# Modulation vectors from unsplit fp32 weights, in four column strips of TensorE

## Chip, cores and metric

One core of a Trainium2 chip runs the whole kernel. The metric is the device time of one execution in microseconds (us). Engines are named as the profile does: PE (TensorE), PEld (its weight loads), DVE (VectorE), ACT (ScalarE), POOL (GpSimd), SP (SyncE, which issues the DMA transfers here).

## What is computed

Two layers over 1024 latent and 256 context tokens of width 1024. Each layer modulates its input by vectors that come from a condition vector `c` (for the latents) and `c_ctx` (for the context), runs attention, a state-space mixer (SSD) and retention side by side, and adds their projection, gated. The part of the reference that matters:

```python
def hybrid_layer(x, ctx, c, c_ctx, w_ada, b_ada, w_in, w_out, ...):
    shift, scale, gate = jnp.split(jax.nn.silu(c) @ w_ada + b_ada, 3, axis=-1)
    ...   # the same for c_ctx; h = rms_norm(x) * (1 + scale) + shift
    ...   # h @ w_in, the mixers, x + gate * (mix @ w_out)
```

`w_ada` is 1024 x 3072 for each of the two layers, in fp32: the product of two vectors (c and c_ctx) with a matrix of 12.6 MB, twice.

## The kernel before

Dense products run with each fp32 operand split into two halves: a rounded one (`hi`, type fp32r, a copy on ACT) and the rest (`lo`, a subtraction on POOL or DVE; `split`, lines 273 to 277). A product then takes three passes, hi x hi, hi x lo and lo x hi (`mm3`, lines 303 and 305).

Weights come in blocks of 256 output columns by 1024 rows (eight contraction tiles of 128). `w_order` writes the order of all blocks by hand, `prefetch` loads the next one, `next_w` hands out the loaded one and asks for the one after it. A block's halves live in tiles `wh` and `wl`, two buffers each. The raw fp32 data come through tiles `raw` (three small buffers), or, for the source marked "gv", through the ring of sixteen large buffers as `wr`; four transfers of 256 KB a block. In the dense stream the splits of a block wait in `pieces` and are let go one at each step of the stream.

The modulation vectors (`ada`, from line 224) are twelve such blocks a layer. The condition is the stationary operand: `sc` holds hi and lo of both vectors as four columns. For each contraction tile `k` and each half `j` of the weights one product of 4 by 256 is accumulated (line 234, sixteen a block); the 4 x 256 result is copied to `adar` on DVE; two small products with `pick` add the four rows in pairs and turn columns into partitions (line 240); one DVE instruction adds the bias (line 243).

In the opening (`run`) the eight blocks of layer 0's shift and scale are made in the order ADA0, and the first chunk of 512 tokens is normalised between them: `norm_h` needs the shift and scale of each feature tile `k` (hu, line 442; ah, line 449; al, line 450, the last also on DVE). Then come the first dense products (`first_dense`), and with them the second chunk of x. The other sixteen blocks (gate of layer 0, all of layer 1) run in the dense stream of layer 0, as LATE says, between weight blocks 10 and 22. The stream is interleaved with the mixers by budgets (SHARE), in which an ada block counts 2.0. Within this order a planner that simulates the engines sets the final order of instructions on each engine, the DMA issues on SP's queue among them.

In the SSD mixer, `pair_stage2` (line 778) multiplies in plain fp32, without a split: two heads alternate, one writing PSUM partitions 0 to 63, the other 64 to 127.

Of the kernel before, what the change touches and what calls it, by code (L numbers as in the profile page):

```python
# [9 lines left out]
F32 = mybir.dt.float32  # L10
# [8 lines left out]
P = 128  # L19
# [21 lines left out]
LAG = 2  # L41
LATE = (1, 0, 1, 3, 2, 2, 2, 2, 1, 1, 1, 1, 3)
PJ = 1
PN = 3
ADA0 = (0, 4, 1, 5, 2, 6, 3, 7)

# [6 lines left out]
class Net:  # L53
# [25 lines left out]

# [1 line left out]
    def nm(self, s):  # L81
# [26 lines left out]

# [1 line left out]
    def copy(self, out, in_, eng=None):  # L110
# [41 lines left out]

# [1 line left out]
    def setup(self):  # L154
# [52 lines left out]

# [1 line left out]
    def silu_c(self):  # L209
        nc = self.nc  # L210
        cc = self.work("cc", (P, KT, 2))
        nc.sync.dma_start(out=cc, in_=self.a["cc"])
        th = self.work("cth", (P, KT, 2))
        nc.scalar.activation(out=th, in_=cc, func=AF.Tanh, scale=0.5)
        nc.vector.scalar_tensor_tensor(out=th, in0=th, scalar=1.0, in1=cc, op0=ALU.add, op1=ALU.mult)
        nc.vector.tensor_scalar(out=th, in0=th, scalar1=0.5, scalar2=None, op0=ALU.mult)
        self.sc = self.const("sc", [P, KT, 4], F32R)
        nc.vector.tensor_copy(out=self.sc[:, :, 0:2], in_=th)
        nc.vector.tensor_tensor(out=self.sc[:, :, 2:4], in0=th, in1=self.sc[:, :, 0:2].bitcast(F32), op=ALU.subtract)
        self.pick = self.const("pick", [4, 2])  # L220
        nc.vector.tensor_tensor(out=self.pick, in0=self.ident[0:4, 0:2], in1=self.ident[0:4, 2:4], op=ALU.add)

    def ada(self, l, ns):
        nc = self.nc
        cols = self.cc_[l][0]
        if l not in self.ada_t:
            self.ada_t[l] = self.c_p.tile([P, 24, 2], F32, tag=f"ada{l}", name=f"ada{l}")
        out = self.ada_t[l]
        for n in ns:
            w = self.next_w()  # L230
            ps = self.pmm()
            for k in range(KT):
                for j in range(2):
                    nc.tensor.matmul(ps[0:4, 0:256], lhsT=self.sc[:, k, :], rhs=w[j][:, k, :],
                                     start=(k == 0 and j == 0), stop=(k == KT - 1 and j == 1))
            row = self.c_p.tile([4, 256], F32, tag="adar", name=self.nm("adar"))
            self.copy(row[0:4, 0:256], ps[0:4, 0:256], "v")
            pt = self.pst()
            for j in range(2):
                nc.tensor.matmul(pt[:, 2 * j:2 * j + 2], lhsT=row[0:4, j * P:(j + 1) * P], rhs=self.pick,  # L240
                                 start=True, stop=True)
            o = out[:, 2 * n:2 * n + 2, :]
            nc.vector.scalar_tensor_tensor(
                out=o, in0=pt[:, 0:4].rearrange("p (j c) -> p j c", c=2), scalar=1.0 if 4 <= n < 8 else 0.0,
                in1=cols[:, COLS["ba"] + 2 * n:COLS["ba"] + 2 * n + 2].unsqueeze(2).to_broadcast([P, 2, 2]),
                op0=ALU.add, op1=ALU.add)
            yield 2.0

# [1 line left out]
    def load_w(self, src, eng="g"):  # L250
        nc = self.nc
        hi = self.w_p.tile([P, KT, 256], F32R, tag="wh", name=self.nm("wh"))
        lo = self.w_p.tile([P, KT, 256], F32R, tag="wl", name=self.nm("wl"))
        self.stage_w(src, hi, lo, 2, eng)
        return hi, lo

    def stage_w(self, src, hi, lo, m, eng="g"):
# [34 lines left out]

# [1 line left out]
    def mm3(self, ps, wh, wl, ah, al, w_first):  # L294
# [63 lines left out]

# [1 line left out]
    def defer(self, n, fn):  # L360
# [37 lines left out]

# [1 line left out]
    def new_act(self, c):  # L400
# [71 lines left out]

# [1 line left out]
    def conv_evac(self, t, idx, cv, edge, c, n, ps):  # L474
# [377 lines left out]

# [1 line left out]
    def rope(self, x):  # L854
# [189 lines left out]

# [1 line left out]
    def ret_mix(self, pr, last):  # L1046
# [83 lines left out]

# [1 line left out]
    def load_mix(self, c, tiles, cols, scaled):  # L1132
# [112 lines left out]

# [1 line left out]
    def w_order(self, l):  # L1247
        wi, wa = self.a["wi"], self.a["wa"]
        q = [(wa[0, i], "gv") for i in ADA0] if l == 0 else []
        late = iter([(wa[0, i],) for i in range(8, 12)] + [(wa[1, i],) for i in range(12)])  # L1250
        for i in range(N_W):
# [7 lines left out]
    def dense_all(self, l, last, cols, cv, xin):  # L1259
# [14 lines left out]
        for j in range(3):  # L1274
            yield from xz(5 + j, 3 + j)
        late = iter([(0, n) for n in range(8, 12)] + [(1, n) for n in range(12)] if l == 0 else [])

# [88 lines left out]
    def run(self):  # L1366
# [7 lines left out]
        for j, n in enumerate(ADA0):  # L1374
# [3 lines left out]
            if j % 2:  # L1378
                next(h0)
                next(h0)  # L1380
            if j == 4:
                self.load_dt(0)
# [27 lines left out]
def _layout(inp):  # L1410
# [6 lines left out]
    o["cc"] = np.stack([g["c"][0].reshape(KT, P).T, g["c_ctx"].reshape(KT, P).T], -1)  # L1417
    o["wa"] = g["w_ada"].reshape(DEPTH, KT, P, 12, 256).transpose(0, 3, 2, 1, 4)

# [71 lines left out]
```

## Time and profile before

| | us |
|---|---|
| median of 3 runs | 2968.34 |
| lowest and highest | 2963.67, 2970.11 |
| span of the profiled execution | 2963.4 |
| PE busy | 2683.0 |
| DVE busy | 1992.9 |
| ACT busy | 1277.0 |
| POOL busy | 1191.2 |

The span goes from the first to the last instruction of one execution; the page gives no other time of that execution. Busy times of engines overlap. Ends of matmuls are modelled, and they are pipelined, so that starts tell more than ends of what a product costs.

### The profile page before, as it was taken

Reading aid. Unit: us, or ns where it says so; the run is one execution under the profiler, and the core shown is the slowest. Engines: PE = TensorE matmul, PEld = TensorE weight load, DVE = VectorE, ACT = ScalarE, POOL = GpSimd, SP = SyncE. Lnnn points to the kernel's source line nnn. Section 1 sums busy time; section 2 is a strip of 40 time slices with the busy share of each in tenths; the row PEclk is TensorE's granted clock in tenths of the full one; section 3 lists DMA queues with packets and bytes.
Section 4 is the critical chain, followed back from the end, with each engine's and each line's share of the span. In section 5 each row is a group of like instructions: output and inputs, shape, how many; then the busy total and the mean of one; then the engine's idle time right before and its main releaser. Section 6 shows DMA issues by size and latency. Waiting matters only on the chain.

```text
span 2963.4 us, 47064 instructions
## 1 busy us (share of the span) xinstructions
PE 2683.0 (91%) x17708; PEld 2352.7 (79%) x17708; DVE 1992.9 (67%) x4409; ACT 1277.0 (43%) x3297; POOL 1191.2 (40%) x910
## 2 busy tenths in 40 slices
PE   6887988779899989998999989997899999999999
PEld 4666777669788879897878777775798888989887
DVE  7668778765767785657445558888658767665651
ACT  5345555443545454523132345545435444452330
POOL 5546656662423231325240336666531211212550
PEclk8988999889999999999999989998999999999999
DMA  6022222221211111204462122222110100001461
GB/s 236 13 69 81 80 76 67 82 67 43 58 44 52 44 53 29 68 27 122 135 216 79 39 73 79 72 78 72 58 43 15 37 15 22 29 24 36 148 211 60
DMA packets 128339, 211.23 MB, mean 71 GB/s; under 512 B 12080, under 2 KB 53232, under 8 KB 128112
## 3 DMA queue, kind: packets, MB, share of 16 engines
q1 hardware_dynamic: 128112, 208.23, 22.5%
q8 instruction: 139, 2.28, 0.3%
q14 instruction: 88, 0.72, 0.1%
HBM read 172.47 MB, written 35.72 MB: 70 GB/s over the span
## 4 chain that ended last, share of the span: by engine, by line
PE 53%; DVE 13%; issue 5%; ACT 3%; DMA 2%; POOL 1%; SPq 0%; DVEq 0%; POOLq 0%; ACTq 0%
PE mm L303 23%; PE mm L305 13%; PE t L149 4%; PE o L975 4%; PE s L924 4%; DVE mx L926 2%; DVE te L747 2%; PE o L778 1%; ACT e L936 1%; DVE e L954 1%; POOL wl L277 1%; DVE mt L744 1%; PE s L710 1%; DMA raw<-in_wi_dram 1%; DVE mt L752 1%
## 5 line engine op out<-in xcount | busy, mean ns | idle before, releaser
L277 POOL TENSOR_TENSOR wl<-raw,wh 128x512 fp32r<-128x512 f32 x288 | 391.5, 1380 | 705.8 <-ACT wh L275 699.0
L303 PE MATMUL mm<-ah,wh 128*128 128x512 f32 (+1 forms) x1680 | 635.3, 378 | 41.2 <-DVE cv L489 7.6
L303 PE MATMUL mm<-al,wh 128*128 128x512 f32 (+1 forms) x1680 | 626.9, 373 | 1.0 <-DVE al L277 1.0
L303 PE MATMUL mm<-ah,wl 128*128 128x512 f32 (+1 forms) x1680 | 626.2, 373 | 0.0
L305 PE MATMUL mm<-wh,ah 128*128 128x256 f32 x1568 | 455.1, 291 | 17.5 <-DVE zu L357 9.9
L305 PE MATMUL mm<-wl,ah 128*128 128x256 f32 x1568 | 451.1, 288 | 0.3 <-POOL wl L277 0.3
L305 PE MATMUL mm<-wh,al 128*128 128x256 f32 x1568 | 450.1, 287 | 0.0
L303 PEld LDWEIGHTS mm<-ah,wh 128*128 128x128 f32 x1680 | 323.9, 193 | 101.9 <-issue 19.4
L303 PEld LDWEIGHTS mm<-ah,wl 128*128 128x128 f32 x1680 | 323.7, 193 | 52.8 <-issue 2.4
L303 PEld LDWEIGHTS mm<-al,wh 128*128 128x128 f32 x1680 | 324.3, 193 | 51.6 <-issue 2.4
L305 PEld LDWEIGHTS mm<-wh,ah 128*128 128x128 f32 x1568 | 302.4, 193 | 24.0 <-DVE zu L357 10.4
L936 ACT ACTIVATE e<-s,nb 128x512 f32<-128x512 f32 (+1 forms) x384 | 231.8, 613 | 198.3 <-DVE nb L931 197.0
L305 PEld LDWEIGHTS mm<-wl,ah 128*128 128x128 f32 x1568 | 302.9, 193 | 4.3 <-issue 1.2
L305 PEld LDWEIGHTS mm<-wh,al 128*128 128x128 f32 x1568 | 302.8, 193 | 3.0 <-issue 0.9
L926 DVE TENSOR_REDUCE mx<-s 128x1 f32<-128x512 f32 (+1 forms) x400 | 223.1, 586 | 64.3 <-PE s L924 63.2
L275 ACT ACTIVATE wh<-raw 128x512 fp32r<-128x512 f32 x288 | 169.1, 625 | 173.1 <-DMA raw<-in_wi_dram 62.0
L924 PE MATMUL s<-kT,qT 128*128 128x512 f32 (+1 forms) x800 | 218.9, 377 | 10.2 <-ACT e L936 8.7
L750 POOL TENSOR_TENSOR mt<-mt,G 128x512 f32<-128x512 f32 x72 | 117.3, 1632 | 177.1 <-DVE mt L744 168.1
L747 DVE SCALAR_TENSOR_TENSOR te<-R,dtpk,te 128x128 f32<-128x128 f32 x288 | 176.0, 656 | 9.5 <-ACT te L739 9.5
L755 POOL TENSOR_TENSOR R<-R,cv 128x1024 f32<-128x1024 f32 x72 | 177.6, 2468 | 2.9 <-ACT R L754 2.9
L975 PE MATMUL o<-v,aT 128*128 128x128 f32 x1312 | 176.4, 277 | 0.7 <-DVE aT L118 0.5
L975 PEld LDWEIGHTS o<-v,aT 128*128 128x128 f32 x1312 | 165.2, 194 | 4.1 <-DVE aT L118 0.9
(265 smaller groups left out, 5182.1 us busy)
## 6 DMA issues: line engine op xcount, KB each, us to landing
raw<-in_wi_dram SPq DMA_DIRECT2D x176, 256.0 KB
R<-cumd SPq DMA_DIRECT2D x72, 512.0 KB
raw<-in_wa_dram SPq DMA_DIRECT2D x64, 256.0 KB
mr<-mix SPq DMA_DIRECT2D x64, 256.0 KB
wr<-in_wa_dram SPq DMA_DIRECT2D x32, 256.0 KB
raw<-in_wo_dram SPq DMA_DIRECT2D x32, 256.0 KB
x<-xr SPq DMA_DIRECT2D x24, 256.0 KB
mix<-cv SPq DMA_DIRECT2D x8, 640.0 KB
```

The costliest lines, as they stand in the source:

```text
L149: self.nc.tensor.transpose(ps[:, j * P:(j + 1) * P], srcs[i + j], self.ident)
L275: nc.scalar.activation(out=hi, in_=x, func=AF.Copy)
L277: e.tensor_tensor(out=lo, in0=x, in1=hi.bitcast(F32), op=ALU.subtract)
L303: nc.tensor.matmul(ps, lhsT=w, rhs=x, start=st, stop=sp)
L305: nc.tensor.matmul(ps, lhsT=x, rhs=w, start=st, stop=sp)
L747: nc.vector.scalar_tensor_tensor(out=te[:, hh, c, :], in0=Rv[:, 1, hh, c, :], scalar=col(self.ncum, c, 1, hh), in1=te[:, hh, c, :], op0=AL ...
L750: nc.gpsimd.tensor_tensor(out=mt, in0=mt, in1=G[:, c0:c0 + 2, :].unsqueeze(1).to_broadcast([P, 2, 2, P]), op=ALU.mult)
L755: nc.gpsimd.tensor_tensor(out=cs, in0=cs, in1=cT[:, tk].unsqueeze(1).to_broadcast([P, 4, 256]), op=ALU.mult)
L924: nc.tensor.matmul(ps[:, 0:n], lhsT=qT[:, 2 * m + s, :], rhs=kT[m][:, t0:t0 + n], start=(s == 0), stop=(s == 1))
L926: nc.vector.tensor_reduce(out=mx[:, ci:ci + 1], in_=ps[:, 0:n], axis=AX.X, op=ALU.max, negate=len(chunks) == 1)
L936: nc.scalar.activation(out=em[:, t0:t0 + n], in_=pss[ci][:, 0:n], func=AF.Exp, bias=nb, accum_out=z[:, 3 * m + ci:3 * m + ci + 1])
L975: nc.tensor.matmul(po[:, 0:P], lhsT=aT[j], rhs=v[:, j, :], start=(j == b0), stop=(j == NT - 1))
```

## The change

The weights of the modulation vectors are no longer split. `load_a` brings a block of 512 columns straight into the buffers of `wh` (contraction tiles 0 to 3) and `wl` (4 to 7), as plain fp32, in four transfers of 512 KB. `sc` holds the two vectors in fp32, padded with zeros to 32 columns. For each half `j` four products go to the four column strips of the array: strip `g` takes contraction tile 4j + g and writes PSUM partitions 32g to 32g + 31. The 128 x 512 result is copied to SBUF, into the ring of work tiles, and four small products with a 128 x 2 `pick` add the strips and turn columns into partitions. There are six blocks a layer in place of twelve; four in the opening, eight in the stream, of which LATE places one at a time. A block counts 2.5 in the budgets. In the opening four feature tiles of h follow each second block.

```diff
-LATE = (1, 0, 1, 3, 2, 2, 2, 2, 1, 1, 1, 1, 3)
+LATE = (1, 0, 1, 1, 1, 1, 1, 1, 1, 0, 0, 0, 0)
-ADA0 = (0, 4, 1, 5, 2, 6, 3, 7)
+ADA0 = (0, 2, 1, 3)
...
-        self.sc = self.const("sc", [P, KT, 4], F32R)
-        nc.vector.tensor_copy(out=self.sc[:, :, 0:2], in_=th)
-        nc.vector.tensor_tensor(out=self.sc[:, :, 2:4], in0=th, in1=self.sc[:, :, 0:2].bitcast(F32), op=ALU.subtract)
-        self.pick = self.const("pick", [4, 2])
+        self.sc = self.const("sc", [P, KT, 32])
+        nc.vector.memset(self.sc, 0.0)
+        nc.vector.tensor_scalar(out=self.sc[:, :, 0:2], in0=th, scalar1=0.5, scalar2=None, op0=ALU.mult)
+        self.pick = self.const("pick", [P, 2])
...
-            for k in range(KT):
-                for j in range(2):
-                    nc.tensor.matmul(ps[0:4, 0:256], lhsT=self.sc[:, k, :], rhs=w[j][:, k, :],
-                                     start=(k == 0 and j == 0), stop=(k == KT - 1 and j == 1))
-            row = self.c_p.tile([4, 256], F32, tag="adar", name=self.nm("adar"))
-            self.copy(row[0:4, 0:256], ps[0:4, 0:256], "v")
+            for j in range(2):
+                for g in range(4):
+                    nc.tensor.matmul(ps[32 * g:32 * g + 32, :], lhsT=self.sc[:, 4 * j + g, :], rhs=w[j][:, g, :],
+                                     start=(j == 0), stop=(j == 1))
+            row = self.work("adar")
+            self.copy(row, ps, "v")
             pt = self.pst()
-            for j in range(2):
-                nc.tensor.matmul(pt[:, 2 * j:2 * j + 2], lhsT=row[0:4, j * P:(j + 1) * P], rhs=self.pick,
+            for j in range(4):
+                nc.tensor.matmul(pt[:, 2 * j:2 * j + 2], lhsT=row[:, j * P:(j + 1) * P], rhs=self.pick,
                                  start=True, stop=True)
...
-            yield 2.0
+            yield 2.5
...
     def load_w(self, src, eng="g"):
+        if eng == "ada":
+            return [self.load_a(src, j) for j in range(2)]
...
+    def load_a(self, src, j):
+        t = self.w_p.tile([P, 4, 512], F32, tag=("wh", "wl")[j], name=self.nm("wa"))
+        for g in range(0, 4, 2):
+            self.nc.sync.dma_start(out=t[:, g:g + 2, :], in_=src[:, 4 * j + g:4 * j + g + 2, :])
+        return t
...
-        q = [(wa[0, i], "gv") for i in ADA0] if l == 0 else []
-        late = iter([(wa[0, i],) for i in range(8, 12)] + [(wa[1, i],) for i in range(12)])
+        q = [(wa[0, i], "ada") for i in ADA0] if l == 0 else []
+        late = iter([(wa[0, i], "ada") for i in (4, 5)] + [(wa[1, i], "ada") for i in range(6)])
...
             if j % 2:
-                next(h0)
-                next(h0)
-            if j == 4:
+                for _ in range(4):
+                    next(h0)
+            if j == 2:
```

## Rows read from the trace of the kernel before

**Rows 1.** The page, part 1: busy us, share of the span, instructions.

```profile
PE 2683.0 (91%) x17708; PEld 2352.7 (79%) x17708; DVE 1992.9 (67%) x4409; ACT 1277.0 (43%) x3297; POOL 1191.2 (40%) x910
```

**Rows 2.** Stretches of the opening: busy per engine, granted clock, DMA share, GB/s.

```profile
12.00:32.00 20.00, 14.77 (x87) 9.09 (x88) 18.52 (x29) 12.37 (x21) 16.00 (x11) 0.91 1.02 356
36.00:40.00 4.00, 2.58 (x22) 1.58 (x20) 4.00 (x8) 3.59 (x7) 1.51 (x2) 1.00 0.68 201
44.00:48.00 4.00, 2.88 (x12) 0.89 (x10) 3.88 (x8) 2.98 (x8) 2.52 (x2) 0.50 0.77 236
48.00:52.00 4.00, 3.13 (x14) 1.82 (x15) 4.00 (x5) 3.68 (x7) 2.84 (x2) 0.50 0.88 254
```

**Rows 3.** Timeline of the opening: start, us, engine, line, operation, out<-in, count.

```profile
29.69 7.69 SPq L263 DMA_DIRECT2D wr<-in_wa_dram  x7
...
57.47 0.28 PE L234 MATMUL mm<-wl,sc 128*4 128x256 f32 x1
...
60.17 1.39 DVE L442 SCALAR_TENSOR_TENSOR hu<-x,ada,s 128x512 f32<-128x512 f32 x2
...
62.09 1.40 DVE L450 SCALAR_TENSOR_TENSOR al<-hu,ada,ah 128x512 fp32r<-128x512 f32 x2
...
66.42 0.62 ACT L410 ACTIVATE acc<-x 128x512 f32<-128x512 f32 x1
```

**Rows 4.** Line 234, 600 to 1260 us: its products; what ended PE's idle time.

```profile
L234 PE MATMUL mm<-wh,sc x128: 276/277/418, 629.3 to 1240.3; 128*4 128x256 f32 x128
...
  DVE zu L357: 11.4, 2
  POOL wl L277: 4.4, 4
...
  ACT wh L275: 2.2, 3
```

**Rows 5.** The stretch of the stream, columns as in group 2.

```profile
700.00:1260.00 560.00, 528.12 (x3796) 480.17 (x3796) 391.45 (x897) 282.99 (x820) 172.69 (x119) 0.97 0.17 50
```

**Rows 6.** Timeline at 18 to 22 us: transposing products, norm sums, one block's products.

```profile
18.67 0.60 PE L240 MATMUL t<-pick,adar 4*128 4x2 f32 x4
...
19.20 1.05 PE L427 MATMUL t<-ones,acc 128*128 128x1 f32 x8
...
20.11 0.28 PE L234 MATMUL mm<-wl,sc 128*4 128x256 f32 x1
...
21.82 0.28 PE L234 MATMUL mm<-wh,sc 128*4 128x256 f32 x1
```

**Rows 7.** Timeline at 310 and 336 us: plain fp32 products in two strips.

```profile
310.16 0.32 PE L778 MATMUL o<-R,st 128*64 128x128 f32 x1
...
310.16 0.32 PE L778 MATMUL o<-mt,xn 128*64 128x128 f32 x1
...
310.32 0.27 PE L778 MATMUL o<-R,st 128*64 128x128 f32 x1
...
336.12 0.39 PE L778 MATMUL o<-mt,xn 128*64 128x128 f32 x4
...
336.34 0.39 PE L778 MATMUL o<-R,sf 128*64 128x128 f32 x4
...
336.88 0.19 PEld L303 LDWEIGHTS mm<-ah,wh 128*128 128x128 f32 x1 [0.17 <-issue]
```

**Rows 8.** 600 to 1260 us: POOL's subtractions by group; ACT's waits before its copies.

```profile
L277 POOL TENSOR_TENSOR wl<-raw,wh 128x512 fp32r<-128x512 f32 x112 | 152.4, 1380 | 319.9 <-ACT wh L275 315.0 <-PE s L924 2.9 <-DMA raw<-in_wa_dram 1.7
...
  DMA raw<-in_wa_dram: 24.4, 22
```

**Rows 9.** DVE copies from PSUM: ns min/median/max of adar; group of aT.

```profile
L118 DVE COPY adar<-mm x16: 402/409/413, 633.3 to 1240.7; 4x256 f32<-4x256 f32 x16
...
L118 DVE COPY aT<-t 128x512 f32<-128x512 f32 x64 | 43.9, 686 | 35.9 <-PE t L149 35.4
```

**Rows 10.** DMA of the first 62 us: packets, bytes, mean rate.

```profile
DMA packets 11236, 17.49 MB, mean 282 GB/s; under 512 B 1760, under 2 KB 3680, under 8 KB 11232
```

More of the change, by code (lines that the diff above doesn't have):

```diff
@@ L215, in silu_c @@
         nc.vector.scalar_tensor_tensor(out=th, in0=th, scalar=1.0, in1=cc, op0=ALU.add, op1=ALU.mult)
-        nc.vector.tensor_scalar(out=th, in0=th, scalar1=0.5, scalar2=None, op0=ALU.mult)
-        self.sc = self.const("sc", [P, KT, 4], F32R)
-        nc.vector.tensor_copy(out=self.sc[:, :, 0:2], in_=th)
-        nc.vector.tensor_tensor(out=self.sc[:, :, 2:4], in0=th, in1=self.sc[:, :, 0:2].bitcast(F32), op=ALU.subtract)
-        self.pick = self.const("pick", [4, 2])
-        nc.vector.tensor_tensor(out=self.pick, in0=self.ident[0:4, 0:2], in1=self.ident[0:4, 2:4], op=ALU.add)
+        self.sc = self.const("sc", [P, KT, 32])
+        nc.vector.memset(self.sc, 0.0)
+        nc.vector.tensor_scalar(out=self.sc[:, :, 0:2], in0=th, scalar1=0.5, scalar2=None, op0=ALU.mult)
+        self.pick = self.const("pick", [P, 2])
+        nc.vector.tensor_reduce(out=self.pick, in_=self.ident.rearrange("p (g c) -> p c g", g=4)[:, 0:2, :],
+                                axis=AX.X, op=ALU.add)
     def ada(self, l, ns):
@@ L231, in ada @@
             ps = self.pmm()
-            for k in range(KT):
-                for j in range(2):
-                    nc.tensor.matmul(ps[0:4, 0:256], lhsT=self.sc[:, k, :], rhs=w[j][:, k, :],
-                                     start=(k == 0 and j == 0), stop=(k == KT - 1 and j == 1))
-            row = self.c_p.tile([4, 256], F32, tag="adar", name=self.nm("adar"))
-            self.copy(row[0:4, 0:256], ps[0:4, 0:256], "v")
+            for j in range(2):
[4 more added lines that the diff above has]
+            self.copy(row, ps, "v")
             pt = self.pst()
-            for j in range(2):
-                nc.tensor.matmul(pt[:, 2 * j:2 * j + 2], lhsT=row[0:4, j * P:(j + 1) * P], rhs=self.pick,
+            for j in range(4):
+                nc.tensor.matmul(pt[:, 2 * j:2 * j + 2], lhsT=row[:, j * P:(j + 1) * P], rhs=self.pick,
                                  start=True, stop=True)
-            o = out[:, 2 * n:2 * n + 2, :]
             nc.vector.scalar_tensor_tensor(
-                out=o, in0=pt[:, 0:4].rearrange("p (j c) -> p j c", c=2), scalar=1.0 if 4 <= n < 8 else 0.0,
-                in1=cols[:, COLS["ba"] + 2 * n:COLS["ba"] + 2 * n + 2].unsqueeze(2).to_broadcast([P, 2, 2]),
+                out=out[:, 4 * n:4 * n + 4, :], in0=pt[:, 0:8].rearrange("p (j c) -> p j c", c=2),
+                scalar=1.0 if 2 <= n < 4 else 0.0,
+                in1=cols[:, COLS["ba"] + 4 * n:COLS["ba"] + 4 * n + 4].unsqueeze(2).to_broadcast([P, 4, 2]),
                 op0=ALU.add, op1=ALU.add)
-            yield 2.0
+            yield 2.5
     def load_w(self, src, eng="g"):
-        nc = self.nc
+        if eng == "ada":
+            return [self.load_a(src, j) for j in range(2)]
         hi = self.w_p.tile([P, KT, 256], F32R, tag="wh", name=self.nm("wh"))
@@ L1275, in dense_all @@
             yield from xz(5 + j, 3 + j)
-        late = iter([(0, n) for n in range(8, 12)] + [(1, n) for n in range(12)] if l == 0 else [])
+        late = iter([(0, n) for n in (4, 5)] + [(1, n) for n in range(6)] if l == 0 else [])
         def more(i):
@@ L1417, in _layout @@
     o["cc"] = np.stack([g["c"][0].reshape(KT, P).T, g["c_ctx"].reshape(KT, P).T], -1)
-    o["wa"] = g["w_ada"].reshape(DEPTH, KT, P, 12, 256).transpose(0, 3, 2, 1, 4)
+    o["wa"] = g["w_ada"].reshape(DEPTH, KT, P, 6, 512).transpose(0, 3, 2, 1, 4)
     def cols(*ranges):
```

## Prediction

> **What bounds the kernel now.** I read the page first: TensorE (PE) is busy 2683 of 2963.4 us, far ahead of VectorE (DVE) with 1993, ScalarE (ACT) with 1277 and GpSimd (POOL) with 1191 [rows 1]. The work that changes stands in two places with different limits, so I read each by itself.
>
> The first is the opening, up to about 63 us, where eight modulation blocks are made, on which the first chunk's dense products wait. The table by stretches shows the loads at 356 GB/s from 12 to 32 us, but at 201 to 254 in the three stretches shown between 36 and 52 us, where DVE is busy nearly all the time and the granted clock falls to 0.5 (the 1.2 GHz level) [rows 2]. The timeline tells why: the last load of modulation weights is issued at 37.4 us, but the last of their products ends at 57.75, and the last of the eight normalised tiles of the first chunk (al, line 450) at 63.5 [rows 3]. So for some 20 us the data are there, and the splits into two halves on ACT, DVE and POOL, the one ring of buffers behind them, and a PE at half clock set the pace. That is no DMA limit.
>
> The second is 629 to 1240 us, where the other sixteen blocks run in the dense stream beside the mixers [rows 4]. From 700 to 1260 us PE is busy 528 of 560 us at a granted clock of 0.97 [rows 5]. There a microsecond of PE work saved is about a microsecond of time, and ACT and POOL work saved is worth only the PE waits that it causes.
>
> **The change, part by part.** The profile's span is 2963.4 us; the runs shown have a median of 2968.3 and a lowest of 2963.7, so some time up to 7 us lies around or beside the profiled execution, and I carry the difference that I work out over to the median.
>
> *Products in the stream, removed.* An old block is 16 products of 256 columns; the sixteen that start from 20.11 to 21.82 stand 1.71 / 15 = 0.114 us apart, so a block is 1.82 us. Two transposing products follow, which the trace shows as four records: 0.53 us from their start to the next instruction's, 18.67 to 19.20 [rows 6]. Sixteen blocks: 16 x 2.35 = 37.6 us of PE.
>
> *Products in the stream, added.* Eight new blocks of eight plain fp32 products, 32 weight columns by 512. No such product is in the trace. The nearest are those of line 778: plain fp32, 64 weight columns by 128, which alternate between the two halves of the array as the new ones alternate between four strips. Each leaves two records, so two passes. The first passes of the two halves both start at 310.16 and the second at 310.32; in steady state a group of four records follows the last after 0.22 us (336.12, 336.34) [rows 7]. So a pass of 128 columns costs 0.109 us, both halves run at once, and a product does not hold up its neighbour's first pass by its own second. Scaled to 512 columns a pass is 0.436 us; a block in four strips is two rounds of two passes, 4 x 0.436 = 1.74 us. Bounds: 0.9 us if the 0.109 is the loading of 64 weight columns and a pass streams at the pace of the old products, 2 x 0.114 for 512 columns [rows 6]; 16 x 0.436 = 7.0 us if the strips do not overlap. I take 1.74, since line 778 is the only plain fp32 work in strips here. To it I add 0.35 us for going into strips and out again (the next full-array product shows 0.17 us of idle weight loading after line 778, at 336.88 [rows 7]; taken twice), and the four transposing products, now over 128 partitions: eight records, which in line 427, also 128 weight columns by a few, take 0.9 us up to the next start, 19.20 to 20.11 [rows 6]. Eight blocks: 8 x (1.74 + 0.35 + 0.90) = 23.9 us. PE saves 13.7 us.
>
> A rule stands against full overlap. The rows of line 778 show two strips in the time of one [rows 7]. The Trainium skill, "TensorE: Matmul & The Clock Gate", Part 3 (packing small matmuls), states 2.38 times for three column strips, and that matmuls start and end strictly in program order. By the first figure four strips would overlap 3.2-fold, an estimate of 2.2 us a block and 2940 us in all; the second, if a product's two passes count as neighbours in the program, is rival B below. On the order, the trace disagrees for two strips: both first passes start together; no run here shows four.
>
> *Splits, removed.* In the stream POOL makes 112 subtractions of 1380 ns, of which 64 belong to these blocks (88 us) and each follows a copy on ACT, which stood 24.4 us waiting for their loads [rows 8]. POOL and ACT are not the bound, so this is worth the PE waits ahead of these products that the splits ended: 4.4 us on POOL and 2.2 on ACT. The 11.4 us put down to DVE zu is a wait for a PSUM bank and remains [rows 4]. Gain 6.6 us, between 0 and, if fewer visits meet fewer waits for the bank, 15.
>
> *Evacuation.* The copy grows from 4 x 256 (0.41 us) to 128 x 512 (0.69 us as in aT) [rows 9]; sixteen become eight, so DVE loses 1 us of work. The products of the mixers cover PE's wait for it, since PE is 94% busy there [rows 5], so I cost it at nothing. Uncovered it is 8 x 0.3 = 2.4 us.
>
> *Loads.* The bytes stay. A block now goes straight into the weight buffers, so its transfers on SP's queue wait until PE has left the block before last, and what is behind them there (the next weights, the mixers' stores) waits too. In the stream a block is asked for one weight block ahead, tens of microseconds, against about 6 us for 2.1 MB at 350 GB/s, so this is hidden. If it were not hidden, it would cost up to 8 x 6 us.
>
> *The opening.* The 32 transfers of wa and 8 of x are 10.5 MB; at 356 GB/s [rows 2] they take 29.5 us, from about 3 us on, so the last block lands at 32.5. Two buffers keep the queue filled: a block lands every 5.9 us and its products, at half clock, take 4 x 0.87 = 3.5. The opening moves 17.49 MB in all [rows 10]; half of the other 7 may be put ahead, which gives 42.5; I take 37. Behind it: half a block of products at half clock 1.7 us, copy 0.7, transposing 1.8, sum 0.2 and hops, together 5; then four tiles of h, now together after the last block, 4 x 1.45 us of DVE as hu and al show [rows 3], with the tail 7. The first chunk is ready at 49 instead of 63.5, between 44.5 and 54.5. What is late next is the second chunk of x: it is read at 66.4 (acc) [rows 3], and all 17.49 MB at 356 GB/s end at 52, against a need 14 us earlier than now, also 52. So I take 12 us, between 4 (these loads or the order of the queue bind) and 18.
>
> Sum: 13.7 + 6.6 + 12 = 32.3 us; 2968.3 - 32.3 = **2936 us**.
>
> **The rivals.** A, the forecast. Its own range: 18 + 13.7 + 15, and the 7 us by which a block's lower bound (0.9) undercuts 1.74 over eight, so 54 us (2914), to 4 + half of 13.7 + 0 (2957).
>
> B, two strips at a time: if the passes go out in program order, a block takes nine slots of 0.436, 3.9 us. Eight blocks with the rest cost 8 x 5.2 = 41.6 us, 4 more than now, which the waits return; in the opening a block at half clock takes 7.9 us, more than the 5.9 of its load, so the opening gains 3. Result 2963, no change. Against it: the two first passes that start together.
>
> C, strips one after another (they share one stream of operands): 8 x (7.0 + 1.25) = 66 us, 28 more than now, less 6.6 of waits; in the opening four blocks of 14 us at half clock end at 70 us instead of 57.75, 12 later. Result 3001, slower. It decides from where the eight products of a block cost over 3.45 us: that is what two old blocks (4.7) less switching and transposing (1.25) leave. Against it: line 778. For it: four strips ask for twice the operands that two did, and no row shows that rate.
>
> D, the gain is made and handed back: the order on every engine is planned anew for the whole program, x comes late in the opening, or the mixers' chains, not PE, set the stream. The opening's 4 and half of 13.7, less some 6 for a worse order: 2963.
>
> **How the numbers follow.** A 0.65, B 0.13, C 0.11, D 0.11. Differences of 0.2% (6 us) are about what a measurement of this kernel can tell from no change. C is slower and D may be by a little: 0.12. Within 0.2%: most of B and D and the slow end of A, 0.15. Faster: 0.73. The range takes A, B and most of D, 2912 to 2966.
>
> **What would show it.** In the profile after: rounds of four records of line 234's successor within some 10 ns, 0.44 us apart at full clock (B: pairs; C: singles); its PE time in the stream about 2 us a block; no wr or raw tile of in_wa, 112 - 64 = 48 POOL subtractions between 600 and 1260 us; the first dense product with the last h tile near 49 us; loads above 300 GB/s up to 40 us. The forecast is wrong if the strips overlap less than twofold, if PE idle rises in the stream by what its work falls, or if the opening still ends after 58 us.

## The result, and the profile after

The changed kernel takes 2937.24 us (median; 2934.35 to 2938.81), against 2969.05 for the kernel before on the same chip: a ratio of 0.990, 95% interval [0.9885, 0.9914]. Predicted were 2936. The profiled execution has a span of 2932.5 us, 30.9 less than before.

In the first part of the page (busy time, share of the span, instructions by engine) every engine has less work than in [rows 1]; GpSimd's falls most, by a tenth:

```profile
PE 2655.7 (91%) x17516; PEld 2323.2 (79%) x17516; DVE 1940.6 (66%) x4368; ACT 1224.5 (42%) x3201; POOL 1074.6 (37%) x830
```

Where the 30.9 us arise can be followed along instructions that both kernels have. The second chunk's first accumulation (acc) starts at 55.4 instead of 66.4 us: 11.0. At the store of the fifth pair of SSD heads 13.3 are gained, 474.9 against 488.2. From there to the end of layer 0, the stage that holds the modulation blocks of the stream, come 17.6 more. Layer 1 adds nothing. The table by stretches shows that stage (length, then busy time and instructions of PE, PEld, DVE, ACT, POOL, then clock, DMA share, GB/s). Before:

```profile
core 0: us, PE busy (x) PEld busy (x) DVE busy (x) ACT busy (x) POOL busy (x), PEclk, DMA share, GB/s
488.18:1544.23 1056.05, 965.02 (x6750) 870.75 (x6750) 702.61 (x1529) 456.73 (x1260) 407.22 (x309) 0.96 0.24 72
```

After:

```profile
474.85:1513.34 1038.49, 944.81 (x6622) 850.33 (x6622) 674.12 (x1510) 419.92 (x1193) 316.41 (x245) 0.95 0.23 73
```

PE's busy time falls by 20.2 us; its idle time, 91.0 and 93.7 us, doesn't fall. DVE loses 28.5 us of busy time with 19 instructions fewer, more than those instructions held: its copies, casts and reductions each take the same time to within 1 us, and the fall lies in TENSOR_TENSOR and SCALAR_TENSOR_TENSOR, which read two tensors (498.5 us before, 469.5 after). It is the first hint of a term that the prediction lacked.

The opening, which answers [rows 2]:

```profile
12.00:32.00 20.00, 16.25 (x78) 6.11 (x80) 8.75 (x28) 2.75 (x5) 0.00 (x0) 0.91 0.99 361
36.00:40.00 4.00, 3.75 (x22) 1.58 (x23) 2.15 (x9) 1.72 (x5) 0.53 (x1) 1.00 1.05 385
40.00:44.00 4.00, 4.00 (x22) 3.15 (x20) 3.96 (x4) 3.22 (x6) 3.88 (x4) 1.00 1.05 387
44.00:48.00 4.00, 0.77 (x3) 0.24 (x2) 3.96 (x8) 2.68 (x5) 1.55 (x1) 1.00 1.06 380
48.00:52.00 4.00, 3.42 (x9) 2.47 (x10) 3.12 (x5) 0.40 (x1) 0.00 (x0) 0.63 0.64 205
```

In these stretches the loads run at 361 to 387 GB/s up to 48 us, where the kernel before fell to 201 to 254. PE has next to nothing to do from 44 to 48 us, and its granted clock in the stretch behind that is 0.63. The timeline says why (start, duration, engine, line, operation, tiles, count, idle time before it and what ended it), where [rows 3] stood before:

```profile
23.36 3.77 SPq L261 DMA_DIRECT2D wa<-in_wa_dram  x6
...
36.24 1.91 PE L234 MATMUL mm<-wa,sc 128*32 128x512 f32 x12
...
39.47 6.08 POOL L284 TENSOR_TENSOR wl<-wr,wh 128x512 fp32r<-128x512 f32 x4 [39.04 <-ACT wh L282]
...
40.28 0.95 PE L240 MATMUL t<-pick,adar 128*128 128x2 f32 x8
40.93 3.50 DVE L284 TENSOR_TENSOR wl<-wr,wh 128x512 fp32r<-128x512 f32 x2
...
44.35 0.15 DVE L242 SCALAR_TENSOR_TENSOR ada<-t,cols 128x8 f32<-128x8 f32 x1
44.54 2.72 DVE L449 SCALAR_TENSOR_TENSOR hu<-x,ada,s 128x512 f32<-128x512 f32 x4
...
47.18 0.68 DVE L284 TENSOR_TENSOR wl<-wr,wh 128x512 fp32r<-128x512 f32 x1
...
49.04 2.07 DVE L457 SCALAR_TENSOR_TENSOR al<-hu,ada,ah 128x512 fp32r<-128x512 f32 x3
```

The last load is issued near 27 us instead of 37.4, the last modulation product ends at 38.15 instead of 57.75, and the last transposing product at 41.2. But the sum behind it (L242) waits until 44.35, because VectorE is busy with splits of the first dense weights. The last tile al ends at 51.1 instead of 63.5. Note the subtraction wl: two of them take 3.50 us while GpSimd is at work (39.47 to 45.55), and one takes 0.68 at 47.18, when it isn't.

A block of the stream, in strips. One row a round: the first record of each round of four, then the next full-array product:

```profile
1012.74 0.64 PE L234 MATMUL mm<-wa,sc 128*32 128x512 f32 x4
...
1013.19 1.04 PE L234 MATMUL mm<-wa,sc 128*32 128x512 f32 x8
1013.62 1.04 PE L234 MATMUL mm<-wa,sc 128*32 128x512 f32 x8
1014.05 0.61 PE L234 MATMUL mm<-wa,sc 128*32 128x512 f32 x4
1014.59 0.50 PE L931 MATMUL s<-kT,qT 128*128 128x512 f32 x1
```

Four records lie within 0.02 us of each other, a round follows the last after 0.43 to 0.45 us, and the block takes 1.85 us from its start to the next product's. So four strips work at once, fully. And of the 112 subtractions on GpSimd [rows 8] 52 are left between 600 and 1260 us (48 were forecast; over the whole stage GpSimd has 64 instructions fewer, 245 against 309):

```profile
L284 POOL TENSOR_TENSOR wl<-raw,wh 128x512 fp32r<-128x512 f32 x52 | 71.1, 1387 | 244.4 <-ACT wh L282 244.1 <-POOL rs L1080 0.4
```

### The profile page after: what moved, and what is told of

It reads as the page before. It is cut to its first block, busy times and chain, and to the rows that moved or that the text cites. A ratio compares the mean times of both kernels' runs of the same rounds, so it can differ in the third digit from the quotient of the medians.

```text
span 2932.5 us, 46241 instructions
## 1 busy us (share of the span) xinstructions
PE 2655.7 (91%) x17516; PEld 2323.2 (79%) x17516; DVE 1940.6 (66%) x4368; ACT 1224.5 (42%) x3201; POOL 1074.6 (37%) x830
## 4 chain that ended last, share of the span: by engine, by line
PE 67%; DVE 21%; issue 4%; ACT 3%; DMA 3%; POOL 2%; SPq 0%; DVEq 0%; POOLq 0%; ACTq 0%
PE mm L310 29%; PE mm L312 17%; PE t L149 4%; PE o L982 4%; PE s L931 4%; DVE te L754 4%; PE o L785 2%; DVE mt L759 2%; DVE mx L933 2%; DVE mt L751 1%; PE s L717 1%; POOL mt L757 1%; ACT e L943 1%; DVE e L961 1%; DVE sf L727 1%
## 5 line engine op out<-in xcount | busy, mean ns | idle before, releaser
L310 PE MATMUL mm<-ah,wh 128*128 128x512 f32 (+1 forms) x1680 | 637.1, 380 | 52.1 <-DVE xr L1168 15.2
L284 POOL TENSOR_TENSOR wl<-raw,wh 128x512 fp32r<-128x512 f32 x224 | 301.7, 1367 | 581.1 <-ACT wh L282 580.6
L282 ACT ACTIVATE wh<-raw 128x512 fp32r<-128x512 f32 x224 | 129.8, 623 | 186.6 <-DMA raw<-in_wi_dram 77.7
L931 PEld LDWEIGHTS s<-kT,qT 128*128 128x128 f32 x800 | 134.2, 193 | 40.7 <-ACT e L943 26.4
```

Source lines behind the costliest of these rows:

```text
L282: nc.scalar.activation(out=hi, in_=x, func=AF.Copy)
L284: e.tensor_tensor(out=lo, in0=x, in1=hi.bitcast(F32), op=ALU.subtract)
L310: nc.tensor.matmul(ps, lhsT=w, rhs=x, start=st, stop=sp)
L931: nc.tensor.matmul(ps[:, 0:n], lhsT=qT[:, 2 * m + s, :], rhs=kT[m][:, t0:t0 + n], start=(s == 0), stop=(s == 1))
```

## The experiments

Differences below are (ratio to the kernel before - 1) x 2968 us, and against the changed kernel (0.990) the difference of two such ratios. "Stage" is always the stretch from the fifth pair's store to the end of layer 0; some expectations speak of a shorter one, from the seventh pair's store.

Two things limit what a difference says. A stage is read from one profiled execution: the three kernels with dummies (below) have the order of the changed kernel on every engine up to 510 us, and yet their second chunk starts at 53.3 to 54.8 us against 55.4, and their stage at 476.9 to 477.8 against 474.9. So 2 or 3 us between two traces say nothing. And the planner writes the order of the whole program anew for every edit, so that a run measures an edit together with its new order.

| | median us | ratio, 95% | stage us | PE busy | DVE busy |
|---|---|---|---|---|---|
| before | 2969.1 | 1 | 1056.1 | 965.0 | 702.6 |
| after | 2937.2 | 0.9900 [0.9885, 0.9914] | 1038.5 | 944.8 | 674.1 |
| open_only | 2967.6 | 1.0001 [0.9985, 1.0016] | 1074.7 | 973.1 | 700.9 |
| open_only_own_row | 2956.8 | 0.9969 [0.9958, 0.9981] | 1058.5 | 964.9 | 699.8 |
| stream_only | 2946.5 | 0.9923 [0.9900, 0.9946] | 1035.7 | 942.5 | 674.8 |
| ring_row | 2985.8 | 1.0070 [1.0052, 1.0088] | 1078.5 | 974.6 | 698.1 |
| two_strips | 2942.8 | 0.9911 [0.9882, 0.9940] | 1046.7 | 960.0 | 677.4 |
| one_strip | 2967.5 | 0.9997 [0.9984, 1.0011] | 1058.3 | 980.3 | 672.5 |
| strip_pairs | 2939.6 | 0.9916 [0.9899, 0.9932] | 1044.7 | 950.4 | 677.7 |
| dummy_splits | 2976.4 | 1.0031 [1.0017, 1.0045] | 1079.5 | 961.3 | 701.6 |
| dummy_free | 2954.0 | 0.9956 [0.9941, 0.9972] | 1054.7 | 952.9 | 699.5 |
| dummy_act | 2943.0 | 0.9917 [0.9891, 0.9944] | 1042.1 | 951.8 | 669.8 |
| row_in_w | 2925.8 | 0.9861 [0.9846, 0.9877] | 1034.4 | 945.7 | 670.2 |
| pool_first | 2939.4 | 0.9908 [0.9891, 0.9925] | 1038.4 | 941.5 | 676.0 |

**The opening alone, and the stream alone.** Each takes the change in one place and the old blocks in the other.

```
open_only:    late blocks of the stream: split, 4 x 256 row
              row = self.work("adar")         # in the ring of eight work tiles
stream_only:  eight blocks of the opening: split, through "wr"
              row = self.work("adar")
```

> Only the opening is changed (four unsplit blocks of 512 columns in strips); the sixteen late blocks run as before, split and with 16 products of 256 columns (their row of results now lies in the ring of work tiles). Theory (opening and stream gain independently, the opening by no longer waiting for splits): 11 to 13 us under the kernel before, about 2957 us, with the last tile of h near 51 us. Rival (what is gained in the opening is given back at a later wait, and the whole gain lies in the stream): within 5 us of before. Rival (the opening gives all of it): within 5 us of the changed kernel, 2937 us.

> Only the stream is changed (eight late blocks in strips); the eight blocks of the opening are split and made as before. Theory: 17 to 20 us under the kernel before, about 2950 us, last tile of h near 63 us. Rival (the opening gives nearly all): within 5 us of before, 2969 us. If the sum of the gains of this run and of the run that changes only the opening is within 5 us of the 32 us of the whole change, the two parts are independent.

The stream alone gave 23 us. The opening alone gave nothing: acc of the second chunk came at 56.2, so the 10 us were won, but the stage lost 18.6 against before. My version of the old blocks differed from the original in one place: their 4 x 256 row lay in the ring of eight work tiles, not in a buffer of its own. The next two runs take that apart.

**The row in its own buffer, and the kernel before with the row in the ring.**

```
open_only_own_row:  - row = self.work("adar")
                    + row = self.c_p.tile([4, 256], F32, tag="sc", ...)
ring_row (before):  - row = self.c_p.tile([4, 256], F32, tag="adar", ...)
                    + row = self.work("adar")
```

> As the run that changes only the opening, but the 4 x 256 row of results of the late split blocks has a buffer of its own again, as before, and no place in the ring of eight work tiles. That run kept the opening's 10 us until 900 us and lost 20 us in the stream. Theory 1 (the row in the ring, held until its transposing products run, stalls the mixers): the stream is as long as before, 955 us from the seventh pair's store to the end of layer 0, and the whole is 9 to 12 us under the kernel before. Theory 2 (the order that the planner writes for split late blocks behind a shifted opening is worse by itself): still within 5 us of the kernel before.

> The kernel before with one edit: the 4 x 256 row lies in the ring of work tiles. Theory 1 (the ring is the cause): 10 to 20 us slower than the kernel before, all of it between 600 and 1540 us. Theory 2 (it is the planner's order behind the shifted opening): within 5 us of the kernel before.

With its own buffer the opening's gain stays, 9 us. And the kernel before loses 21 us (interval 15 to 26) by an edit of nothing but the place of a 4 KB row: its stage takes 22.4 us longer, with as many instructions. PE's busy time there isn't work alone: it is 9.6 us longer for as many records (6750), at a granted clock of 0.94 against 0.96.

```profile
490.17:1568.63 1078.46, 974.57 (x6750) 879.97 (x6750) 698.07 (x1530) 456.87 (x1260) 409.23 (x309) 0.94 0.23 70
```

The ring hands out its tiles in turn, to the mixers' qT, khl and aT too, so a row that stays until PE has transposed it holds up a place in the mixers' chain. That this is the path of the loss is argued; that the place costs the time is shown. A rival path is the planner's order: in ring_row it differs from that of the kernel before on every engine (on VectorE from the 39th instruction on), and no run holds it fixed. Against chance in the order speaks that the ring is the slower place in all three pairs of runs, by 21 us here, 9 between the two open_only kernels and 12 in row_in_w below. The changed kernel has its rows there as well, eight in the stream and four in the opening. Opening (9) and stream (23) make 32, the whole change 30, the same within the intervals; stream_only's old blocks in the opening also have their rows in the ring (its second chunk starts at 69.9 us, against 66.4), so 23 may be a little low.

**Two strips, and one.** They keep everything but the number of strips (copy and transposing products then take 64 or 32 partitions), and so put known amounts of PE work back.

```
- nc.tensor.matmul(ps[32 * g:32 * g + 32, :], ..., start=(j == 0), stop=(j == 1))
+ nc.tensor.matmul(ps[32 * (g % 2):32 * (g % 2) + 32, :], ...)     # two_strips
+ nc.tensor.matmul(ps[0:32, :], ...)                               # one_strip
```

> The changed kernel, but the four contraction tiles of a half go to two column strips in turn instead of four. Theory (PE work in the stream is time): a block takes 8 passes one after another of 0.43 us, 3.4 us in place of 1.75, so eight late blocks cost 13 to 14 us; the opening loses 2 to 6 us, since a block at half clock takes 7 us against 5.9 us of its load: 2952 to 2958 us. Rival (the stream gains by the freed ACT and POOL alone, PE products run in gaps): within 4 us of the changed kernel, 2937 us.

> The changed kernel, but all eight contraction tiles of a block accumulate in one column strip. Theory: 16 passes of 0.43 us, 6.9 us a block in place of 1.75, so eight late blocks cost 41 us; the opening becomes bound by PE, 4 to 28 us later by the clock that it gets: 2982 to 3006 us, slower than the kernel before. Rival (the strips don't matter, unsplit weights do): within 10 us of the changed kernel, 2937 to 2947 us.

Two strips, a block: pairs 0.45 us apart, 3.56 us to the next product.

```profile
881.42 0.62 PE L234 MATMUL mm<-wa,sc 128*32 128x512 f32 x2
...
881.87 1.03 PE L234 MATMUL mm<-wa,sc 128*32 128x512 f32 x4
...
884.45 0.60 PE L234 MATMUL mm<-wa,sc 128*32 128x512 f32 x2
884.98 0.33 PE L149 MATMUL t<-ident,e 128*128 128x128 f32 x1
```

One strip: single records 0.43 to 0.45 us apart, 6.98 us.

```profile
896.78 0.62 PE L234 MATMUL mm<-wa,sc 128*32 128x512 f32 x1
...
897.23 1.02 PE L234 MATMUL mm<-wa,sc 128*32 128x512 f32 x2
...
903.24 0.59 PE L234 MATMUL mm<-wa,sc 128*32 128x512 f32 x1
903.76 0.33 PE L149 MATMUL t<-ident,e 128*128 128x128 f32 x1
```

The blocks cost about what rivals B and C had said of them (3.9 and 7.0), yet I had expected too much of the time: 3 us (by the medians 6) and 29 more than four strips. The stages show the price of PE work here:

```profile
474.19:1520.84 1046.65, 959.99 (x6622) 853.10 (x6622) 677.40 (x1510) 419.94 (x1193) 314.86 (x245) 0.95 0.23 72
```

```profile
483.16:1541.41 1058.25, 980.25 (x6622) 855.99 (x6622) 672.50 (x1510) 420.30 (x1193) 316.24 (x244) 0.96 0.22 71
```

With two strips PE is busy 15.2 us longer and the stage 8.2, with one strip 35.4 and 19.8. A microsecond of PE's busy time is 0.54 and 0.56 us of time here, or 0.60 and 0.48 if the work is taken from the blocks, 8 x 1.71 and 8 x 5.13 us; one trace each gives no more than: about half. The rest goes into idle time that was there, which falls from 93.7 to 86.7 and 78.0 us. In the opening one strip cost only 5.2 us (acc at 60.6): PE was busy 19.36 of the 20 us from 12 to 32, at a granted clock of 1.00 against 0.91 with four strips, so the half clock on which rival C had reckoned did not come.

**The two products of a strip one after the other.**

```
- for j in range(2):
-     for g in range(4):
+ for g in range(4):
+     for j in range(2):
```

> The changed kernel with the two halves of a strip one behind the other: strip 0 with contraction tiles 0 and 4, then strip 1 with 1 and 5, and so on, in place of strips 0 to 3 and again 0 to 3. If PE begins products only in the order of the program, the second product of a strip waits for both passes of the first and holds up the next strip, and a block goes from 1.85 us towards 5 us: 8 x 3 us of PE, half of it time, 8 to 16 us over the changed kernel. If each strip has a queue of its own that lets a later strip go ahead, the starts look as before and the time is within 4 us of the changed kernel.

The time is that of the changed kernel within the intervals (4.7 us more by the ratios). The second product in the program now belongs to the strip that the first still keeps busy for 0.43 us or more. All the same four first passes start within 0.04 us: four records end 0.04 us after one would.

```profile
878.13 0.62 PE L234 MATMUL mm<-wa,sc 128*32 128x512 f32 x1
...
878.13 0.66 PE L234 MATMUL mm<-wa,sc 128*32 128x512 f32 x4
```

The records don't name their strip, but one strip's passes stand 0.43 us apart (one_strip), so these are in four strips: if the order is that of the edit, products of later strips went ahead of an earlier one that had to wait. Whether the planner kept that order, the opening shows, where a block's transfers, of two contraction tiles each, land one after another. The changed kernel starts two products on the first transfer:

```profile
13.01 1.07 PE L234 MATMUL mm<-wa,sc 128*32 128x512 f32 x2 [13.01 <-DMA wa<-in_wa_dram]
```

strip_pairs starts one, whose two passes stand 0.82 us apart, and three more at once when another transfer is there:

```profile
12.31 1.89 PE L234 MATMUL mm<-wa,sc 128*32 128x512 f32 x2 [12.31 <-DMA wa<-in_wa_dram]
14.78 1.08 PE L234 MATMUL mm<-wa,sc 128*32 128x512 f32 x3 [0.58 <-DMA wa<-in_wa_dram]
```

So the next strip's product, whose data had come with the first one's, was held up by one that waited for its load: the first strip's second product does stand ahead of it. A product that waits for a load stops those behind it; one that waits for its strip doesn't. In the stream the order can't be read, but first passes stand 13 ns apart there, against 7 in the changed kernel, as if one product were passed over each time.

**The splits' load, put back.** Sixty-four copies on ScalarE and as many subtractions on GpSimd, whose results nobody reads. First on the weight tiles themselves, then on the identity, which no load waits for, then the copies alone.

```
+ d = self.w_p.tile([P, 512], F32, tag="raw", ..., bufs=RAW)
+ nc.scalar.activation(out=d, in_=x, func=AF.Copy)
+ nc.gpsimd.tensor_tensor(out=d, in0=x, in1=d, op=ALU.subtract)   # not in dummy_act
  # x: dummy_splits a quarter of the weight tile; dummy_free, dummy_act the identity
```

> The changed kernel with the split work of the eight late blocks put back as a load without a purpose: 64 copies of 128 x 512 on ACT and 64 subtractions on POOL, spread over the steps of the stream as before, their results unread, so that PE never waits for them. Two and one strips added 15 and 36 us of PE busy time to the stream and made it 8 and 20 us longer, so about half of PE work is time there, and the 13.7 us that PE saves explain some 7 of the 16 us by which the stream is shorter. Theory A (the other 9 us are the freed ACT and POOL): 6 to 10 us over the changed kernel, 2943 to 2947 us. Theory B (they are PE's waits for splits, or the planner's order): within 4 us of the changed kernel.

> The changed kernel (2937.2 us), and for each modulation block of the stream eight more pieces of load on ScalarE and GpSimd: a copy and a subtraction of 4 x 128 each, as many as the splits that the change removed (64 and 64). They read the identity, not the weight tile, and nobody reads what they write, so they wait for no load of weights and keep no weight buffer from being filled; they still pass through the ring of raw tiles. The dummies that read the weight tiles gave 2976 us. Theory 1: what the splits cost was the load on ScalarE and GpSimd itself, which delays the splits of the next weights: 6 to 10 us, 2943 to 2947, with the stage from the seventh pair's store to the end of layer 0 at 944 to 948 us against 938.4. Theory 2: the load is free, and the dummies cost 39 us only because they held the weight buffers: 2937 to 2940, the stage within 2 us of 938. Theory 3: the ring of raw tiles is what costs, and it is still shared here: 2960 to 2976.

> The changed kernel (2937.2 us) with the 64 free dummy copies on ScalarE alone; the 64 subtractions on GpSimd are left out. With both, the time was 2954.0 us, and in the stage from the seventh pair's store to the end of layer 0 VectorE was busy 614.8 us against 595.0 for the same instructions (the subtractions khl, 128 x 256, took 684 ns against 445). Theory 1: GpSimd's subtractions hold up VectorE's instructions, and that is what the load costs: without them 2937 to 2942, khl back at 420 to 480 ns, VectorE busy 589 to 601 us in the stage. Theory 2: ScalarE's copies delay the exponentials and the evictions of the mixers: 2948 to 2954 with VectorE's durations back at those of the changed kernel. Theory 3: neither engine, but the place in the ring of raw tiles, which the next weights wait for: 2950 to 2954 with khl at 445, and POOL waiting longer for loads of weights.

The first cost 39 us, but mixed two things: it also reads the weight buffers, which can't be filled again until it has. With that taken out the load costs 17 us (10 to 23), more than twice what I had given the splits. The copies alone leave 5, which the intervals can't tell from nothing. So most of it is GpSimd's: 12 us, though with an interval of 2 to 21. The stage of dummy_free and that of dummy_act:

```profile
477.78:1532.49 1054.71, 952.91 (x6622) 854.77 (x6622) 699.46 (x1510) 453.51 (x1257) 403.45 (x308) 0.94 0.22 72
```

```profile
476.93:1519.05 1042.12, 951.83 (x6622) 854.39 (x6622) 669.84 (x1510) 454.43 (x1257) 316.48 (x245) 0.95 0.23 73
```

VectorE has the same 1510 instructions in both and in the changed kernel, but with GpSimd's subtractions they take 699.5 us instead of 669.8 or 674.1. Of the 29.6 us between the two runs 26.0 lie in TENSOR_TENSOR and SCALAR_TENSOR_TENSOR, 3.8 in TENSOR_SCALAR, and none in copies, casts and reductions. One of them, the mixers' subtraction khl (of each group: count, busy us, mean ns, idle us before). In the kernel before and the changed one:

```profile
L277 DVE TENSOR_TENSOR khl<-k,khl 128x256 fp32r<-128x256 f32 x16 | 10.0, 637 | 0.8 <-ACT khl L275 0.8
```

```profile
L284 DVE TENSOR_TENSOR khl<-k,khl 128x256 fp32r<-128x256 f32 x16 | 6.8, 445 | 1.1 <-ACT khl L282 1.1
```

with the free dummies, and with their copies alone:

```profile
L292 DVE TENSOR_TENSOR khl<-k,khl 128x256 fp32r<-128x256 f32 x16 | 10.7, 684 | 1.5 <-ACT khl L290 1.5
```

```profile
L291 DVE TENSOR_TENSOR khl<-k,khl 128x256 fp32r<-128x256 f32 x16 | 6.4, 418 | 1.1 <-ACT khl L289 1.1
```

The timeline of the kernel before shows it happen:

```profile
783.81 3.86 POOL L277 TENSOR_TENSOR wl<-raw,wh 128x512 fp32r<-128x512 f32 x2
...
786.92 2.45 DVE L277 TENSOR_TENSOR khl<-k,khl 128x256 fp32r<-128x256 f32 x2
...
787.83 1.26 POOL L277 TENSOR_TENSOR wl<-raw,wh 128x512 fp32r<-128x512 f32 x1 [0.16 <-ACT wh L275]
...
788.10 0.63 PE L149 MATMUL t<-ident,khl 128*128 128x128 f32 x4 [1.20 <-DVE khl L277]
```

Two khl take 2.45 us where 0.84 would do. The first ends 0.3 us after GpSimd's instruction (783.81 + 3.86 = 787.67), the second 0.3 us after the next one (789.09), and PE waits 1.20 us. Of the sixteen khl of this stage four took 1.04 to 1.50 us in the kernel before, one 0.84 in the changed kernel, six 0.74 to 1.48 in dummy_free and none over 0.43 in dummy_act; every long one lies beside an instruction of GpSimd. The Trainium skill, "SBUF — State Buffer", section "SBUF: two separate sides", states that VectorE and GpSimd share a pair of ports by an exclusive lock, that a VectorE instruction with two SBUF inputs needs it, and that whoever comes second is blocked for the whole instruction. The trace agrees: khl has two inputs and waits GpSimd out, while the copy adar, which reads PSUM, takes 679 ns in dummy_free, where four of the eight lie beside an instruction of GpSimd, and 682 in the changed kernel. That GpSimd lengthens VectorE's instructions is shown; that the 12 us all come by way of VectorE isn't. From dummy_act to dummy_free PE's waits put down to VectorE grow by 5.0 us, to ScalarE by 3.9, and to GpSimd itself, whose other results come later too, by 3.6.

**The row somewhere else.** The products that read a weight buffer have ended when the row is copied, so it can lie there.

```
- row = self.work("adar")
+ row = w[0][:, 0, :]
```

> The changed kernel (2937.2 us) with one thing moved: the 128 x 512 row of the four partial sums is copied into the weight buffer whose products have just ended, not into the ring of work tiles. In the kernel before, moving the row into that ring cost 18 us for sixteen rows. Theory 1: each visit to the ring delays the chain of tiles that runs there, and eight visits cost half of sixteen: 2937 less 6 to 10, so 2927 to 2931. Theory 2: the ring cost the kernel before only because sixteen rows met it there with PE, the splits and the ring all late; with eight it has slack: 2935 to 2939. Theory 3: the weight buffer is now held about 2 us longer by the transposing products, and the next load starts as much later: in the opening 2 buffers of 8 blocks give 2 to 8 us more, 2939 to 2945.

2925.8 us: 12 us less than the changed kernel (the intervals, [0.9846, 0.9877] and [0.9885, 0.9914], don't meet), and the fastest of all. In the profile it is 8.4 us: 1.9 before the second chunk, no more than traces of one order differ, 4.1 in the stage, and some 2 to 3 in layer 1, where no row lies. So the time is won by the edit with its new order; how much of it is the ring's own doing stays open.

```profile
473.23:1507.61 1034.38, 945.65 (x6622) 849.20 (x6622) 670.17 (x1512) 420.08 (x1192) 316.41 (x244) 0.96 0.23 73
```

**VectorE freed in the opening.** The first dense weights are split on GpSimd alone, so that the sum L242 finds VectorE free.

```
- self.split(raw, hi..., lo..., eng[k // m % len(eng)])
+ self.split(raw, hi..., lo..., eng[k // m % len(eng)] if self.alive_once else "g")
```

> The changed kernel (2937.2 us) with the splits of the first weight blocks of layer 0 all on GpSimd instead of half on VectorE. In the opening of the changed kernel VectorE splits dense weights from 38.6 to 44.4 us while the sum of the last modulation block waits there for its turn, although its transposing products end at 41.2. Theory 1: with VectorE free the sum starts near 41.5 and the first chunk's last h tile ends 2 to 3 us earlier, at 48 to 49 us, and this stays in the total: 2934 to 2935. Theory 2: GpSimd then ends the splits later than VectorE and GpSimd together (four pieces more of 1.4 us) and the first dense products wait for them instead: 2937 to 2941, with the h tiles early and PE still idle at 48 us.

The sum starts at 39.23 instead of 44.35, the last al ends at 48.2 instead of 51.1, and the second chunk's acc starts 5.4 us earlier (3.3 to 4.7 against the kernels with dummies, which have the changed kernel's order there). At 98 us 4 are left (2 to 4), at 285 us none. Nearly half of the first gain was lost at once, beside GpSimd, as khl's was: four al take 5.84 us there, where three took 2.07 in the changed kernel.

```profile
41.19 8.14 POOL L285 TENSOR_TENSOR wl<-wr,wh 128x512 fp32r<-128x512 f32 x5
```

```profile
42.35 5.84 DVE L458 SCALAR_TENSOR_TENSOR al<-hu,ada,ah 128x512 fp32r<-128x512 f32 x4
```

What took the rest between 98 and 285 us I have not settled.

## Why the prediction was right, step by step

The total was right to 1 us of the median, and so was the forecast's mechanism for the strips and the opening. Two of the four terms were mis-sized, and one that I had set to nothing was not; they offset each other. That the total came out to 1 us is therefore luck in good part.

*Products in the stream.* Four strips at once: right, as the rows of line 778 had it [rows 7]. A pass takes 0.43 us as scaled (0.436), the block 1.85 us where I had 1.74 + 0.35 = 2.09. So 16 x 2.35 - 8 x (1.85 + 0.90) = 15.6 us by rows, 20.2 in the stage's PE busy time; predicted 13.7. Wrong was the sentence that a microsecond of PE work saved is about a microsecond of time there, taken from 528 busy of 560 us [rows 5]. Two strips and one show about half. If that slope holds downwards too, 15.6 to 20.2 us of work are 8 to 11 us of time. A busy share near one is no proof of such a price: here the remaining idle time took up half of what PE was given.

*Splits.* The step that failed: worth "the PE waits that it causes", by the releasers in the rows of waits, 6.6 us, at most 15 [rows 4]. Put back, the load costs 17 us (16.2 in the stage). The rows of waits name who came last, POOL wl and ACT wh; they don't say that VectorE, which other rows name (khl), was late because GpSimd had held it up. The change removed 64 subtractions from GpSimd, and VectorE became faster. I also misread the rows that I went by. [rows 4] adds up the waits of PE and those of its weight loads (PEld), which are the same waits seen twice. PE's own, between 600 and 1260 us:

```profile
PE mm L234 <- DVE zu L357: 5.6, 1, 5.6
...
PE mm L234 <- POOL wl L277: 1.8, 1, 1.8
...
PE mm L234 <- ACT wh L275: 0.8, 1, 0.8
```

By its own rule the term was 2.6 us, not 6.6, and still further from what the load costs. These waits are gone: in the changed kernel the products wait for zu alone, 8.3 us.

*Evacuation.* I asked for the copy's duration (0.69 us predicted, 0.68 measured) and for PE's wait, and costed it at nothing. The cost is in where the row lies. The old row had a buffer of its own; the new one takes a place in the ring of work tiles. Such rows, eight in the stream and four in the opening, cost 4 us in the stage by row_in_w and 12 in the whole time; by half of ring_row's sixteen it would be 11 in the stage. I had no row for it, so its bounds should have been open on both sides.

*The opening.* Predicted 12, measured 11.0 in the trace (acc) and 9 alone. The first chunk ended at 51.1, not 49. I had the loads right (361 GB/s and more in the stretches shown up to 48 us), and wrong what is late next: not x, but VectorE, which has splits of the first dense weights ahead of the last sum.

Together for the stage: -11 to -8 (PE work), -16 (splits), +4 to +11 (row) make -23 to -13; measured -17.6. With the opening's 11.0 and 2.3 between the two it is 30.9. That the terms add up so is worked out from separate runs, each with an interval of several microseconds, not measured in one. Nor is it a closed account: nobody waits for the dummies' results, so the 16 don't hold the 2.6 us of direct waits, which are gone too, while PE's idle time as a whole didn't fall (91.0 and 93.7).

*The rivals.* B's blocks exist as two_strips, 3.56 us instead of 3.9, but at 2943, not 2963; C's as one_strip, 6.98 us as predicted, at 2967, not 3001. The point from which C decides, 3.45 us a block, was wrong for the same reason, and left out what the freed GpSimd gives: even at 6.98 us a block the new kernel is no slower than the old. Rival D, gains handed back by a new order, happened in the experiments (open_only lost 18.6 us in the stage behind a gain of 10; pool_first kept nothing of 5.4), but not in the change itself, whose stage kept 17.6. In open_only the loss went with the place of the row, in pool_first the cause stays open.

## What to carry to other kernels

Before costing work removed from GpSimd, compare the shortest and the mean duration of VectorE's two-input instructions in the same stretch: what lies between them is what GpSimd may be taking from VectorE, if the long ones lie beside its instructions, and the rows of waits showed it here under VectorE's name. It isn't yet time: 26 us of it went with a cost of 12. Read the waits of a line engine by engine, so that a wait of PE isn't counted again for its weight loads. Ask of each tile that a change adds or moves which ring it takes a place in and who else waits for that ring; here this cost 12 us for twelve rows, and the weight buffer just consumed was a free place. And test the price of the busiest engine's time by adding a known amount of work to it, rather than reading it off the busy share.

## What the runs showed of the hardware

Four plain fp32 products of 32 weight columns by 512 run in four column strips with no loss: rounds of four records 0.43 to 0.45 us apart, just as single records in one strip. A product that waits for its strip doesn't hold up later products for other strips (strip_pairs: four first passes within 0.04 us), while one that waits for its load does (12.31 and 14.78 us). A VectorE subtraction of two 128 x 256 tensors takes 0.42 us alone and up to 1.50 us beside GpSimd's subtractions.

The first of these goes beyond the figure of the Trainium skill that the prediction weighed ("TensorE: Matmul & The Clock Gate", Part 3, 2.38 times for three strips): here four strips give 6.98 / 1.85 = 3.8 times, the switch to the next product included. The same part of the Trainium skill states that matmuls start and end strictly in program order; the second differs from that for products in different strips, and the measurement decides.
